# Four staging buffers for the memory keys and one junk tile of their own for the samples' scores

## Chip, cores and metric

The kernel runs on one core of a Trainium2 chip. The metric is the device time of one execution in microseconds (us). Three runs of the kernel before took 849.76, 850.98 and 851.43 us; their median, 850.98 us, is the time before.

## What is computed

One decoder layer for a prompt of 512 tokens and 8 samples of one token each, so 520 columns in all. Three sub-layers follow each other: a mixer (mLSTM and retention heads), a cross-attention of 4 heads into 256 memory tokens, and a SwiGLU feed-forward. The change touches the cross-attention. There, the prompt attends to keys and values that are made from `mem_prompt` in this kernel and are outputs too; each sample attends to its own cached keys and values, which come from memory.

```
def mem_kv(mem, g_mem, w_ck, w_cv):
    mn = rmsnorm(mem, g_mem)
    k = (mn @ w_ck).reshape(B, N_MEM, X_HEADS, X_HEAD_DIM)
    v = (mn @ w_cv).reshape(B, N_MEM, X_HEADS, X_HEAD_DIM)
    return k, v

def cross_attn(x, mk, mv, w_cq, w_co):
    q = (x @ w_cq).reshape(B, T, X_HEADS, X_HEAD_DIM)
    s = jnp.einsum('bthd,bmhd->bhtm', q, mk) * (X_HEAD_DIM ** -0.5)
    p = jax.nn.softmax(s, axis=-1)
    o = jnp.einsum('bhtm,bmhd->bthd', p, mv).reshape(B, T, D_MODEL)
    return o @ w_co
```

## The kernel before

Activations lie feature-major: 128 features on the partitions, 520 columns, 8 blocks of 128 features. Every float32 operand of a matmul is split into a rounded part (hi, by ScalarE) and the rest (lo, by VectorE), and each product is three matmuls (hi·hi, hi·lo, lo·hi). Weights come in 140 pieces of up to 512 KB through `wload`: SyncE loads `wraw` (3 buffers), ScalarE casts `whi` (2 buffers), VectorE subtracts `wlo` (2 buffers); for the pieces in `LO_ON_POOL` (52 to 55 and 60 to 71, the first half of the memory values' weights, the later queries' and those of the output projection) GpSimd does the subtraction instead.

The order of the instructions on each engine is not the order of the code: the program is built with a scheduler that simulates a timeline and fixes one order per engine beforehand. On the chip each engine then runs its list in order and waits on semaphores. So a change of buffers, which changes who must wait for whom, also changes the orders.

The cross-attention in the order of the code:

- `queries(h)` makes two blocks of queries (`pcq`, `qf`), and `ask(h)` turns the samples' queries into `Mq`.
- `mem_keys(cb)`, eight times: 24 matmuls into PSUM (`pmk`, one of the two buffers of the pool `acc`), VectorE scales them into the staging tile `kf` (L887), `split` makes KT hi on ScalarE and KT lo on VectorE, and GpSimd issues the DMA that writes `kf` out as the output of the memory keys (L889).
- `mem_values(c)`, twice: 48 matmuls of 512 columns into `pmv` (pool `acc` too).
- `samples()`, a coroutine beside all this: for every cached tile (`kv`, 512 KB, 3 buffers, loaded by SyncE) a unit `keys` or `values`. A unit has two matmuls that spread a query or a weight row over the partitions (`pq` or `pw`, one of four PSUM buffers of the tag `msc`, which `pxs`, `ppT`, `pxo`, `pst` and `ptq` share in turn), and four VectorE instructions (L953 or L967, each followed by the read of its accumulator) that multiply tile and row and keep only the sum; the product itself goes to a junk tile `jk` that nobody reads. There are 32 units, 16 of keys and 16 of values. After four keys of a head, `exps` transposes the scores (`pst`, L975), makes the softmax and, in `samples`, the rows `Mp` (L194) that the values of that head need. After four values, a split of `sv` writes the sample columns of `B` (hi on ScalarE, lo on VectorE, L191).
- `heads()` does the prompt's attention (`pxs`, `ppT`, `pT`, `pxo`), and the passes of the output projection (`pwc`, L222) add into `X` (L1128, the last pass L295). The first pass needs the rows of heads 0 and 1 in `B`, the second those of head 2, the third those of head 3, each with the samples' columns.

The staging tile and the junk tiles share one tag in the pool `cp`, whose tiles have two buffers unless told otherwise: `kf` in `mem_keys`, `jk` (`sjk`) in `keys` and `jk` (`svj`) in `values` take turns in two buffers.

```
kf = cp.tile([P, NM], F32, tag="kf", name="kf")          # mem_keys
jk = cp.tile([P, XD], F32, tag="kf", name="sjk")         # keys
jk = cp.tile([P, NM], F32, tag="kf", name="svj")         # values
```

Of the kernel before, what the change touches and what calls it, by code (L numbers as in the profile page):

```python
# [10 lines left out]
F32 = mybir.dt.float32  # L11
# [12 lines left out]
P = 128  # L24
# [8 lines left out]
NM = 256  # L33
XD = 256
# [106 lines left out]
def decoder_step(ctx: ExitStack, tc: tile.TileContext, i: dict, o: list):  # L141
# [20 lines left out]
    def ps2(name):  # L162
        return acc.tile([P, 2, 512], F32, tag="acc", name=name)

    def ps1(name):
        return psums[-1].tile([P, 512], F32, tag="msc", name=name)
# [17 lines left out]
    def selb(b):  # L184
        return sel[:, 4 * P + b * P : 4 * P + (b + 1) * P]


    def split(hi, lo, src, scale=None):

        if scale is None:  # L190
            return act.copy(hi, src), dve.tensor_tensor(lo, src, hi.bitcast(F32), ALU.subtract)  # L191
        else:
            act.activation(hi, src, AF.Copy, scale=scale)
            dve.scalar_tensor_tensor(lo, src, scale, hi.bitcast(F32), ALU.mult, ALU.subtract)  # L194
# [18 lines left out]
    def mm3(out, wh, wl, xh, xl, first, last):  # L213
        pe.matmul(out, wh, xh, start=first, stop=False)
        pe.matmul(out, wh, xl, start=False, stop=False)
        pe.matmul(out, wl, xh, start=False, stop=last)
# [15 lines left out]
    def step():  # L232

        for t in list(tasks):
            t[1] -= 1
            if t[1] <= 0:
                try:
                    t[1] = next(t[0]) or 2
                except StopIteration:
                    tasks.remove(t)  # L240
# [583 lines left out]
    cp = cx.enter_context(tc.tile_pool(name="cp", bufs=2))  # L824
# [53 lines left out]
    def mem_keys(cb):  # L878

        hi, lo = W.get()  # L880
        pk = ps2("pmk")[:, 0]
        for k in range(KB):
            mm3(pk[:, :NM], hi[:, k], lo[:, k], memh[:, k], meml[:, k], k == 0, k == KB - 1)
            if k in (2, 5):
                step()
        kf = cp.tile([P, NM], F32, tag="kf", name="kf")
        dve.tensor_tensor(kf, pk[:, :NM], rm_bc, ALU.mult)  # L887
        split(KT[:, 0, cb], KT[:, 1, cb], kf)
        pool.dma_start(mk_o[cb], kf)  # L889
        step()  # L890
# [41 lines left out]
    def cache_tile():  # L932

        while cached and len(loaded) < 3:
            src, h, b2 = cached.pop(0)
            t = cp.tile([P, 4, XD], F32, tag="kv", name="kv", bufs=3)
            sp.dma_start(t, src[h, b2])
            loaded.append(t)
        return loaded.pop(0)
# [3 lines left out]
    def keys(t, sc):  # L943

        kc = cache_tile()
        pq = ps1("pq")
        jk = cp.tile([P, XD], F32, tag="kf", name="sjk")
        for b1 in range(2):
            pe.matmul(pq[:, b1 * XD : (b1 + 1) * XD], selb(t * 2 + b1), Mq, start=True, stop=True)
        for b1 in range(2):  # L950
            b = t * 2 + b1
            for m in range(2):
                dve.tensor_tensor_reduce(  # L953
                    jk, kc[:, b1 * 2 + m], pq[:, b1 * XD : (b1 + 1) * XD], 1.0, 0.0, ALU.mult, ALU.add, sc[:, m, b : b + 1]
                )

    def values(t, sv):

        vc = cache_tile()
        pw = ps1("pw")  # L960
        jk = cp.tile([P, NM], F32, tag="kf", name="svj")
        for b1 in range(2):
            pe.matmul(pw[:, b1 * NM : (b1 + 1) * NM], selb(t * 2 + b1), Mp, start=True, stop=True)
        for b1 in range(2):
            b = t * 2 + b1
            for dd in range(2):
                dve.tensor_tensor_reduce(  # L967
                    jk, vc[:, b1 * 2 + dd], pw[:, b1 * NM : (b1 + 1) * NM], 1.0, 0.0, ALU.mult, ALU.add, sv[:, dd, b : b + 1]
                )
# [14 lines left out]
    def samples():  # L984
# [4 lines left out]
        for t in range(4):  # L989
            keys(t, sc)  # L990
            yield SAMPLES_REST[0]
# [3 lines left out]
        for h, units in enumerate(ORDER):  # L995
            split(Mp[0:8], Mp[32:40], e[0], scale=e[1])
            yield 1
            sc = cp.tile([P, 2, NS], F32, tag="ssc", name="ssc")
            sv = cp.tile([P, 2, NS], F32, tag="sv", name="sv")
            at = {"V": 0, "K": 0}  # L1000
            for z in units:
                while z == "K" and asked[0] <= h:
                    yield 1
                (values if z == "V" else keys)(at[z], sv if z == "V" else sc)
                at[z] += 1
                if z == "V" and at[z] == 4:
                    kb = 2 * h
                    split(B[:, 0, kb : kb + 2, T:], B[:, 1, kb : kb + 2, T:], sv)
                    done[0] = h
                yield SAMPLES_REST[h + 1]  # L1010
                if z == "K" and at[z] == 4:
                    scored[0] = h + 1
                    e = exps(sc)
                    if z == units[-1]:
                        yield 3
# [88 lines left out]
    for cb in range(KB):  # L1104
        mem_keys(cb)
# [289 lines left out]
```

## Time and profile before

| | us |
|---|---|
| median of three runs | 850.98 |
| the profiled execution | 851.71 |
| its span, first to last instruction | 849.9 |
| TensorE (PE) busy | 824.3, 97% of the span |
| VectorE (DVE) busy | 632.8, 74% |
| ScalarE (ACT) busy | 426.5, 50% |
| GpSimd (POOL) busy | 163.0, 19% |

The memory keys are made between 323 and 352 us, the memory values up to 385, the remaining queries up to 418, the output projection up to 481. The profile shows a TensorE clock of 1.00 of full speed in the stretches up to 464 us. A matmul's record is longer than its turn, since matmuls are pipelined: what a row costs is read from one start to the next. In the timelines a number in brackets is the idle time of the engine before a row and who ended it. Buffer numbers are left out of the names there, but the printed orders of the program have them, so that `pq_4851` in an order is one of the `pq` of the timeline.

### The profile page before, as it was taken

What the parts mean: (1) busy time and instruction counts of PE and PEld (TensorE: products, weight loads), DVE (VectorE), ACT (ScalarE), POOL (GpSimd) and SP (SyncE); (2) the same over time, 40 slices, a digit from 0 to 9 for tenths busy, and PEclk for the clock granted to TensorE, in tenths of its full rate; (3) what the DMA queues carried; (4) which work ended last, traced back from release to release, by engine and by line L of the source; (5) the groups of instructions that cost most, each with busy time, mean ns of one, the idle gap of its engine ahead of it and who ended that gap; (6) DMA issues with size and microseconds to landing.
All of it is one profiled execution on the core that took longest, in us unless ns stands there. A gap on an engine that the chain in (4) does not pass through costs nothing.

```text
span 849.9 us, 16985 instructions
## 1 busy us (share of the span) xinstructions
PE 824.3 (97%) x6643; PEld 807.6 (95%) x6643; DVE 632.8 (74%) x1393; ACT 426.5 (50%) x871; POOL 163.0 (19%) x282
## 2 busy tenths in 40 slices
PE   6999999999999999899999899999999999999995
PEld 4999999999999999789999899999999999999995
DVE  5999977667676778767888899999999997422234
ACT  6556886556545544356432555555454455332231
POOL 5122422222145301424322500000000000010010
PEclk9999999999999999999999999999999999999999
DMA  8344546444526347784755222333333333333212
GB/s 279 103 131 164 176 168 217 158 138 162 189 76 216 105 127 246 235 287 130 243 196 153 75 58 93 107 113 90 109 113 118 101 99 94 94 106 94 79 59 100
DMA packets 34088, 119.01 MB, mean 140 GB/s; under 512 B 4320, under 2 KB 6560, under 8 KB 32728
## 3 DMA queue, kind: packets, MB, share of 16 engines
q1 hardware_dynamic: 27216, 95.80, 35.9%
q0 software_dynamic: 5024, 20.79, 6.7%
q10 hardware_dynamic: 1768, 1.34, 0.5%
q8 instruction: 52, 0.85, 0.4%
q14 instruction: 28, 0.23, 0.1%
HBM read 108.77 MB, written 9.14 MB: 139 GB/s over the span
## 4 chain that ended last, share of the span: by engine, by line
PE 86%; DVE 6%; DMA 4%; POOL 1%; ACT 1%; issue 1%; SPq 0%; DVEq 0%; POOLq 0%; ACTq 0%
PE pfd L1277 13%; PE pfb L1236 6%; PE pfa L1236 6%; PE pcv L222 6%; PE pgt L222 5%; PE pcq L222 5%; PE pwo L222 5%; PE ppl L222 5%; PE pwc L222 4%; PE pfd L1236 3%; PE pfe L1236 3%; PE pfc L1236 3%; PE prp L222 3%; PE pfu L222 2%; PE pfg L222 2%; PE pfd L1317 1%
## 5 line engine op out<-in xcount | busy, mean ns | idle before, releaser
L207 ACT CAST whi<-wraw 128x1024 fp32r<-128x1024 f32 (+1 forms) x104 | 107.3, 1033 | 167.3 <-PE pfd L1277 58.1
L208 DVE TENSOR_TENSOR wlo<-wraw,whi 128x1024 fp32r<-128x1024 f32 (+1 forms) x88 | 112.6, 1281 | 71.5 <-ACT whi L207 69.5
L306 POOL TENSOR_TENSOR ssq<-ssq,sq 128x520 f32<-128x520 f32 x18 | 29.1, 1618 | 355.6 <-ACT sq L305 355.5
L191 ACT CAST qhi<-wsum 128x512 fp32r<-128x512 f32 x72 | 42.9, 620 | 41.4 <-DVE wsum L1183 26.6
L1277 PE MATMUL pfd<-TT,whi 128*128 128x260 f32 x392 | 62.8, 283 | 0.0
L1277 PEld LDWEIGHTS pfd<-TT,whi 128*128 128x128 f32 x392 | 53.7, 189 | 0.0
L1236 PE MATMUL pfa<-TT,qhi 128*128 128x260 f32 x288 | 53.1, 282 | 0.0
L1236 PE MATMUL pfb<-TT,qhi 128*128 128x260 f32 x288 | 52.8, 283 | 0.0
L208 POOL TENSOR_TENSOR wlo<-wraw,whi 128x1024 fp32r<-128x1024 f32 x16 | 38.4, 2399 | 60.3 <-ACT whi L207 55.2
L191 DVE TENSOR_TENSOR qlo<-wsum,qhi 128x512 fp32r<-128x512 f32 x72 | 48.9, 683 | 0.6 <-ACT qhi L191 0.6
L222 PE MATMUL pwc<-B,whi 128*128 128x260 f32 x256 | 43.8, 287 | 4.0 <-DVE X L295 3.0
L222 PE MATMUL pcv<-A,whi 128*128 128x260 f32 x256 | 44.3, 293 | 1.7 <-ACT whi L207 1.7
L1236 PEld LDWEIGHTS pfb<-TT,qhi 128*128 128x128 f32 x288 | 44.4, 189 | 0.2 <-issue 0.2
L1236 PEld LDWEIGHTS pfa<-TT,qhi 128*128 128x128 f32 x288 | 44.4, 189 | 0.0
L222 PE MATMUL prp<-A,whi 128*128 128x260 f32 x256 | 44.2, 291 | 0.0
L222 PE MATMUL ppl<-A,whi 128*128 128x260 f32 x256 | 42.9, 287 | 0.0
L222 PE MATMUL pgt<-A,whi 128*128 128x260 f32 x256 | 42.7, 289 | 0.0
L222 PE MATMUL pcq<-A,whi 128*128 128x260 f32 x256 | 42.0, 284 | 0.0
L222 PE MATMUL pwo<-B,whi 128*128 128x260 f32 x256 | 41.4, 283 | 0.0
L1236 PE MATMUL pfb<-TT,qlo 128*128 128x260 f32 x144 | 40.8, 283 | 0.0
L222 PEld LDWEIGHTS pwc<-B,whi 128*128 128x128 f32 x256 | 35.8, 189 | 5.1 <-DVE X L295 3.7
L1236 PE MATMUL pfa<-TT,qlo 128*128 128x260 f32 x144 | 40.5, 282 | 0.0
(431 smaller groups left out, 2556.6 us busy)
## 6 DMA issues: line engine op xcount, KB each, us to landing
wraw<-in_weights_dram SPq DMA_DIRECT2D x132, 512.0 KB, 3.8
kqb<-there POOLq DMA_DIRECT2D x8, 1024.0 KB, 5.2
kv<-in_cache_k_dram SPq DMA_DIRECT2D x16, 512.0 KB, 4.3
kv<-in_cache_v_dram SPq DMA_DIRECT2D x16, 512.0 KB, 4.4
wraw<-in_weights_dram SPq DMA_DIRECT2D x8, 384.0 KB, 3.1
X<-in_x_dram SPq DMA_DIRECT2D x2, 1040.0 KB, 5.9
Cs<-in_state_C_dram POOLq DMA_DIRECT2D x4, 512.0 KB, 4.3
out_dram<-Cs POOLq DMA_DIRECT2D x4, 512.0 KB, 3.0
```

The source lines that it names most:

```text
L191: return act.copy(hi, src), dve.tensor_tensor(lo, src, hi.bitcast(F32), ALU.subtract)
L207: act.copy(hi[:, :n], raw[:, :n])
L208: (pool if index in LO_ON_POOL else dve).tensor_tensor(lo[:, :n], raw[:, :n], hi[:, :n].bitcast(F32), ALU.subtract)
L222: pe.matmul(ps[:m, a, :H2], w[:, k, c0 : c0 + m], x[:, s, xk, a * H2 : (a + 1) * H2], start=first and w is hi and s == 0, stop=last and w ...
L306: (dve if ob == KB - 1 else pool).tensor_tensor(ssq, ssq, s, ALU.add)
L1236: pe.matmul(out, w[:, k * P : (k + 1) * P], x[:, k * H2 : (k + 1) * H2], start=k == 0 and w is wh and x is xh, stop=k == 3 and w is wl,)
L1277: pe.matmul(ps[:, a, :H2], w[:, k - k0], ff(s, k, slice(a * H2, (a + 1) * H2)), start=k == 0 and w is hi and s == 0, stop=k == FB - 1 and ...
L1317: pe.matmul(ps, w[:, k], ff(s, k0 + k, ts), start=k0 + k == 0 and w is hi and s == 0, stop=k0 + k == FB - 1 and w is lo,)
```

## The change

The staging tile `kf` gets four buffers. The junk tiles of both kinds get a tag of their own, `jk`, with one buffer.

```diff
-        kf = cp.tile([P, NM], F32, tag="kf", name="kf")
+        kf = cp.tile([P, NM], F32, tag="kf", name="kf", bufs=4)
...
-        jk = cp.tile([P, XD], F32, tag="kf", name="sjk")
+        jk = cp.tile([P, XD], F32, tag="jk", name="sjk", bufs=1)
...
-        jk = cp.tile([P, NM], F32, tag="kf", name="svj")
+        jk = cp.tile([P, NM], F32, tag="jk", name="svj", bufs=1)
```

No instruction is added or taken away; the orders of all engines change between the third memory key and the end of the output projection. Three places follow. The names: `kf`, `sjk`, `svj`, `KT` as above, `snb`, `spp` and `Mp` belong to the samples' softmax, and what stands in brackets is what the instruction waits for (DMASW: a DMA issued by GpSimd, DMAHW: one issued by SyncE or ScalarE, DVE: VectorE itself).

First place: VectorE at the fifth and sixth memory key, before.

```order
L967 ISA svj_4592,sv_4588<-kv_4407,pw_4591 128x256 [waits DMAHW3_49,DMASW2_49,PE_49]
L967 ISA sv_4588 128x1
L887 TENSOR_TENSOR kf_4605<-pmk_4566,rm_bc_3547 128x256 [waits DMASW3_49]
L208 TENSOR_TENSOR wlo_4659<-wraw_4656,whi_4658 128x1024 [waits DMAHW1_49,Activation_49]
...
L887 TENSOR_TENSOR kf_4641<-pmk_4616,rm_bc_3547 128x256 [waits DMASW4_49]
L953 ISA sjk_4649,ssc_4587<-kv_4464,pq_4648 128x256 [waits DMAHW6_49,DVE_49,PE_49]
```

The same engine with the change, from the seventh key's staging to the first scores behind the eighth:

```order
L887 TENSOR_TENSOR kf_4687<-pmk_4662,rm_bc_3547 128x256 [waits DMASW2_49,PE_49]
L191 TENSOR_TENSOR KT_3545<-kf_4687,KT_3545 128x256 [waits Activation_49]
L967 ISA svj_4592,sv_4588<-kv_4407,pw_4591 128x256 [waits DMAHW3_49,PE_49]
...
L887 TENSOR_TENSOR kf_4733<-pmk_4698,rm_bc_3547 128x256 [waits DMASW3_49,PE_49]
L967 ISA svj_4592,sv_4588<-kv_4407,pw_4591 128x256 [waits DVE_49]
L967 ISA sv_4588 128x1
L967 ISA svj_4592,sv_4588<-kv_4407,pw_4591 128x256 [waits DVE_49]
L967 ISA sv_4588 128x1
L191 TENSOR_TENSOR KT_3545<-kf_4733,KT_3545 128x256 [waits Activation_49]
L953 ISA sjk_4649,ssc_4587<-kv_4464,pq_4648 128x256 [waits DMAHW6_49,DVE_49]
```

A `kf` now waits for the DMA of the fourth one before it, and no score waits for such a DMA. The unit `svj_4592`, which stood between the fourth and the sixth `kf`, stands around the eighth, and the unit `sjk_4649` behind the last KT.

Second place: VectorE at the first values of head 2, before.

```order
L967 ISA svj_5639,sv_5606<-kv_5470,pw_5638 128x256 [waits DMAHW0_49,PE_49]
L967 ISA sv_5606 128x1
L967 ISA svj_5610,sv_5606<-kv_5448,pw_5609 128x256 [waits DVE_49]
L967 ISA sv_5606 128x1
L967 ISA svj_5639,sv_5606<-kv_5470,pw_5638 128x256 [waits DVE_49]
L967 ISA sv_5606 128x1
```

With the change:

```order
L967 ISA svj_5610,sv_5606<-kv_5448,pw_5609 128x256 [waits DVE_49]
L967 ISA sv_5606 128x1
L967 ISA svj_5639,sv_5606<-kv_5470,pw_5638 128x256 [waits DMAHW0_49,DVE_49,PE_49]
L967 ISA sv_5606 128x1
L967 ISA svj_5639,sv_5606<-kv_5470,pw_5638 128x256 [waits DVE_49]
L967 ISA sv_5606 128x1
```

Two units took turns before, so that a score's wait was for a product two scores back; now they stand one behind the other, and every score waits for the one just before it, that of the next unit too.

Third place: TensorE at the last softmax of the samples (`pst_5816`), before.

```order
L222 MATMUL pwc_5890<-B_81,wlo_5762 128x260
L975 MATMUL pst_5816<-cst_85,ssc_5605 8x128
L222 MATMUL pwc_5890<-B_81,wlo_5762 128x260
L222 MATMUL pwc_5890<-B_81,whi_5761 128x260 x3
L975 MATMUL pst_5816<-cst_85,ssc_5605 8x128
L963 MATMUL pw_5827<-Mp_4069,sel_86 128x256 x2
L222 MATMUL pwc_5890<-B_81,whi_5761 128x260
```

With the change:

```order
L222 MATMUL pwc_5947<-B_81,wlo_5762 128x260 x2
L222 MATMUL pwc_5997<-B_81,whi_5886 128x260
L975 MATMUL pst_5816<-cst_85,ssc_5605 8x128 x2
L963 MATMUL pw_5827<-Mp_4069,sel_86 128x256 x2
L963 MATMUL pw_5850<-Mp_4069,sel_86 128x256 x2
L222 MATMUL pwc_6011<-B_81,whi_5886 128x260
L214 MATMUL pxo_5860<-pT_5788,Vm_3546 128x512
```

The second `pst` stood behind 159 matmuls of the output projection; it stands behind 193 now, when the whole first pass (`pwc_5947` is its last block) is issued.

## Rows read from the trace of the kernel before

**Rows 1.** Stretches: busy us of PE, PEld, DVE, ACT, POOL; clock, DMA share, GB/s.

```profile
323.00:352.00 29.00, 26.64 (x214) 25.57 (x213) 23.69 (x59) 12.22 (x20) 5.89 (x8) 1.00 0.77 244
418.00:445.00 27.00, 27.00 (x219) 26.27 (x218) 22.66 (x78) 12.03 (x27) 8.58 (x4) 1.00 0.62 200
```

**Rows 2.** Waits of PE in the whole span: us in total, times, longest.

```profile
PE pwc L222 <- DVE X L295: 3.0, 2, 2.7
PE pmk L214 <- DVE kf L887: 1.6, 2, 1.5
PE pwc L222 <- DVE X L1128: 0.9, 2, 0.7
PE pq L949 <- DVE ssc L953: 0.7, 1, 0.7
```

**Rows 3.** Timeline of PE at the last memory keys: start, us, instruction.

```profile
342.25 0.40 PE L949 MATMUL pq<-Mq,sel 128*128 128x256 f32 x2
342.81 0.39 PE L214 MATMUL pmk<-B,whi 128*128 128x256 f32 x1 [0.16 <-DVE kf L887]
...
345.78 0.40 PE L963 MATMUL pw<-Mp,sel 128*128 128x256 f32 x2
347.65 0.36 PE L214 MATMUL pmk<-B,whi 128*128 128x256 f32 x1 [1.47 <-DVE kf L887]
...
350.48 0.28 PE L216 MATMUL pmk<-B,wlo 128*128 128x256 f32 x1
351.45 0.51 PE L949 MATMUL pq<-Mq,sel 128*128 128x256 f32 x2 [0.70 <-DVE ssc L953]
352.07 0.47 PE L214 MATMUL pmv<-whi,B 128*128 128x512 f32 x1
```

**Rows 4.** Chain that ended last, one piece: start, us, what (matmuls of `pwc`).

```profile
461.03 8.91 PE pwc L222 x72
```

**Rows 5.** Timeline of DVE at the last memory keys.

```profile
347.08 0.42 DVE L887 TENSOR_TENSOR kf<-pmk,rm_bc 128x256 f32<-128x256 f32 x1 [1.72 <-DMA out_dram<-kf]
347.42 0.41 DVE L953 CUSTOM_DVE_ANT_0 sjk<-kv,pq 128x256 f32<-128x256 f32 x1
...
347.87 0.42 DVE L953 CUSTOM_DVE_ANT_0 sjk<-kv,pq 128x256 f32<-128x256 f32 x1
...
348.68 2.38 DVE L191 TENSOR_TENSOR KT<-kf,KT 128x256 fp32r<-128x256 f32 x1
```

**Rows 6.** Timeline of POOL in the same stretch.

```profile
347.80 0.54 POOL L889 DMA_DIRECT2D out_dram<-kf  x1 [4.21 <-DVE kf L887]
348.35 2.42 POOL L208 TENSOR_TENSOR wlo<-wraw,whi 128x1024 fp32r<-128x1024 f32 x1
```

**Rows 7.** Timeline of DVE where two units of values take turns.

```profile
430.69 0.42 DVE L967 CUSTOM_DVE_ANT_0 svj<-kv,pw 128x256 f32<-128x256 f32 x1
...
431.03 0.42 DVE L967 CUSTOM_DVE_ANT_0 svj<-kv,pw 128x256 f32<-128x256 f32 x1
```

**Rows 8.** Timeline of PE: first `pw` of head 2, second `pst` of the last softmax, second pass.

```profile
428.23 0.40 PE L963 MATMUL pw<-Mp,sel 128*128 128x256 f32 x2
...
444.14 0.27 PE L975 MATMUL pst<-cst,ssc 128*8 128x128 f32 x1
...
452.90 0.35 PE L222 MATMUL pwc<-B,whi 128*128 128x260 f32 x1
```

**Rows 9.** Timeline of DVE: last key score to the splits of the outputs.

```profile
441.62 0.42 DVE L953 CUSTOM_DVE_ANT_0 sjk<-kv,pq 128x256 f32<-128x256 f32 x1
...
450.55 0.69 DVE L1128 TENSOR_TENSOR X<-X,pwc 128x520 f32<-128x520 f32 x1
451.16 0.41 DVE L967 CUSTOM_DVE_ANT_0 svj<-kv,pw 128x256 f32<-128x256 f32 x1
...
452.11 0.70 DVE L191 TENSOR_TENSOR B<-sv,B 128x16 fp32r<-128x16 f32 x1
...
463.38 0.17 DVE L191 TENSOR_TENSOR B<-sv,B 128x16 fp32r<-128x16 f32 x1
```

## Prediction

> **What bounds the kernel now.** Read the stretches first [rows 1]: from 418 to 445 us TensorE (PE) is busy all the time, and VectorE (DVE) over eight tenths of it. At the memory keys, 323 to 352 us, PE has free time, 2.4 us of 29. So the chip follows PE's list, and a DVE instruction counts only where PE has to wait for it. The list of PE's waits says where that is [rows 2]: on the staging `kf` 1.6 us, on a sample's score 0.7 us, both at the memory keys, and then on the additions into `X`, 0.9 and 3.0 us, in the output projection.
>
> The timeline of PE at the keys gives the sizes [rows 3]. A matmul's turn is 0.124 us, 72 of them in 8.91 us [rows 4]. From 342.25 to 342.81 two matmuls need 0.25 of 0.56 us; from 345.78 to 347.65 two need 0.25 of 1.87; from 350.48 to 351.45 one needs 0.12 of 0.97; from there to 352.07 two need 0.25 of 0.62. PE loses 0.3 + 1.6 + 0.85 + 0.4 = 3.2 us (rounded). The cause is in DVE's timeline [rows 5]: `kf` stood 1.72 us for a DMA that writes out an earlier `kf`, since two buffers serve `kf` and the junk of the scores. The scores queued behind it ended late, and with them the PSUM buffer that PE's next `pq` takes over.
>
> There is a second chain, that of the samples: scores, softmax, `Mp`, values, split. It meets PE again at the second pass of the output projection. The lo split of head 2's outputs runs from 452.11 to 452.81 us [rows 9], and the next matmul of that pass starts at 452.90 [rows 8]. So in this trace PE is not early there: what it gains before 452 us is worth something only if the samples come earlier too.
>
> **The change, part by part.**
>
> *Four staging buffers.* Each `kf` now waits for the DMA issued four keys before; a key takes PE 24 x 0.124 = 3.0 us, so that DMA is some 12 us old, where one of a single key before came 1.72 us too late [rows 5]. The waits on DMAs go, at the scores too. Upper bound of the gain: the 3.2 us above. Lower bound: nothing, if another wait takes the place at once.
>
> *What is late next.* In the new order the unit `sjk_4649` stands behind the last KT split, and PE takes its PSUM buffer for `pq_4851` after 12 matmuls of the memory values. I follow both with the rows' durations. Without stalls the eighth key ends near 347.7 us, and PE stands at `pq_4851` near 351.2. On DVE the last `kf` follows PE's end, two scores and the KT split follow it, and then four scores at 0.46 us each: the last is done near 351.9. PE waits about 0.7 us, so 2.5 of the 3.2 us are left. Bounds: no wait, and the case of the second rival.
>
> *One junk buffer.* A score that follows another unit's score starts 0.34 us after it (430.69 to 431.03 [rows 7]); one that waits for the write just before it starts 0.46 us after (347.87 less 347.42 is 0.45 [rows 5]). So such a wait costs 0.12 us of DVE. In the order before 27 of the 128 scores follow a score that wrote the same buffer; with the change it is 66, since two units no longer take turns. That is 39 x 0.12 = 4.7 us more on DVE, 19 of the 39 (2.3 us) behind the first values of head 2. What covers them is the free time of DVE, 4.3 us from 418 to 445 [rows 1]; where a score is on the chain of the samples there is no cover. The Trainium skill, in "VectorE: DVE Perf Modes", section "The DRAIN you can't avoid", says that a semaphore between chained VectorE operations costs nothing extra, as the pipe is emptied anyway. The rows here disagree, with 0.34 against 0.45 us. By that page the sum below would be 0.5 us less.
>
> *The order of PE.* The scheduler now puts the samples' work later between PE's matmuls: `pst_5816` stands behind 193 matmuls `pwc`, not 159. PE works through its list, so these 34 x 0.124 = 4.2 us stand before the last softmax, whether its scores are ready or not. Less the 2.5 us gained, the second `pst` comes at 444.14 + 4.2 - 2.5 = 445.8 us [rows 8]. Are the scores of the keys ready then? The first `pw` of head 2 has 17 matmuls more in front, so it comes at 428.23 + 2.1 - 2.5 = 427.8; from there to the last key score DVE took 13.4 us (441.62 less 428.23 [rows 8, 9]), and now 10 waits of 0.12 and one more addition into `X`, 0.6 us (451.16 less 450.55 [rows 9]): 15.2 us, so 443.0. They are ready; PE's list decides.
>
> *From `pst` to the split of head 2's outputs.* Before it took 452.81 - 444.14 = 8.7 us. One addition into `X` and a split of `pT`, 0.6 us each, now stand ahead of it or hide in PE's time: -1.2. Four more waits: +0.5. The split itself, 16 columns wide, took 0.70 us, and the one of the next head 0.17 [rows 9]: -0.5. That gives 7.5 us: the split ends at 453.3, 0.5 us later than before.
>
> *The end.* Behind it, the second pass is the same on PE. The 0.9 us that PE waited there for additions into `X` [rows 2] may go, as PE then comes later than DVE; on the other side, the split of the last head's outputs is put behind the last addition of the pass, so PE waits for an addition and a small split, 0.8 us, less four matmuls that it can do first: +0.4. The third pass and all behind it keep their order, so I take no change there, the waits of 3.0 us [rows 2] included.
>
> Sum: -3.2 + 0.7 (kept at the keys) + 4.2 (order of PE) - 1.2 + 0.5 - 0.5 (shorter chain) - 0.9 + 0.4 = 0.0 us. The whole is a large gain that is handed back. The profiled execution, 851.71 us with a span of 849.9, is 0.7 us above the median of the runs; against the median the forecast is 851.0 us.
>
> **The rivals.**
>
> *The gain stays (faster).* The 4.2 us of PE's order cost nothing if PE really is that much earlier, that is if the samples' chain behind `pst` gets shorter by more than I take: the softmax's steps on ScalarE and DVE find both engines free, and DVE is not held by GpSimd. For it speaks that at the keys the change takes away just the wait that the rows show, and that DVE has free time. Against it: the lo split and PE's next matmul meet at 452.8 us already. The time if 2.7 of the 3.2 us are kept: 848.3 us. It decides if the split of head 2 ends before 451 us.
>
> *The last KT split is held by GpSimd (slower).* At 348.68 this split took 2.38 us; the one of GpSimd's `wlo`, 2.42 us long, had begun at 348.35 [rows 5, 6]. With the change the last KT split stands behind two scores: it is ready about 0.7 us after the end of `kf`. GpSimd issues the DMA of that `kf` (it began 0.3 us after the end of `kf`, and took 0.54 us) and then begins the next `wlo`, about 0.85 us after the end [rows 5, 6]. If GpSimd is first, the KT split and the four scores behind it are late by 2.38 - 0.42 = 2.0 us (0.42 is `kf` itself [rows 5], as wide as the split), and the split before it can lose as much to the `wlo` before. PE then waits at `pq_4851` not 0.7 but 2.7 to 3.5 us; nothing of the gain at the keys is left, and the 4.2 us of PE's order stand unpaid. The sum is then +2.0 to +2.8; I take +2.4: 853.4 us. It decides from the point where PE's gain at the first memory values is under 0.8 us. The margin is 0.15 us, so this is no unlikely case. The Trainium skill, in "SBUF — State Buffer", section "Who interferes with whom", says that a VectorE instruction with two SBUF inputs and a GpSimd instruction that reads SBUF take one shared port by turns and that the one that begins first holds it to its end; the rows agree, the split ended at 351.06, just behind the `wlo` at 350.77.
>
> *The change does nothing.* The waits on the DMAs are gone from the order, so this one is small; its time is the one of before, and it counts to the forecast's side.
>
> **How the numbers follow.** About 0.2% of the time, 1.7 us, is what a measurement of this kernel can tell from no change. The forecast, within 1.7 us of 850.98, has 0.45 with the third rival; the slower rival 0.32; the faster one 0.23. The likeliest gives 851.0 us; its own range, with PE's wait at `pq_4851` between 0 and 2 us and the 0.9 us kept or not, is 849.5 to 852.7. The range for 8 in 10 reaches into both rivals: 849.0 leaves the core of the faster one out, 853.7 takes most of the slower one in.
>
> **What would show it.** Right would be: no PE wait on `kf`; the memory values begin near 348 us and not at 352; a wait of PE on a score at the first chunk of the memory values; the pair of `pst` of the last softmax near 446 us, with a gap of PE behind it, and a split of head 2's outputs that ends near 453 us; from the third pass on the same distances as before. Wrong: the split at 450 us or earlier (the first rival), a KT split of over 2 us behind the last `kf` and a PE wait of 3 us there (the second), or PE waits on `kf` as before (the third).

## The result and the profile after

The change is slower: 862.66 us (858.13 to 868.18, five runs) against 851.15 for the kernel before on the same chip, ratio 1.0129, 95% interval 1.0099 to 1.0158. The forecast was 851.0, its range ended at 853.7.

The profiled execution took 861.76 us, 10.05 more than that of before. TensorE (PE) begins the memory keys 1.6 us later, at 324.69 and not 323.08; ahead of that its order is the same in both, and over all profiled runs below this start lies anywhere between 320.9 and 326.7 us, so I don't put it down to the change. From there to the first matmul of the feed-forward part (`pfg`, at 480.99 before, 491.40 after) it is 157.9 us before and 166.7 after: **8.8 us are lost in this stretch**. Behind it the two are equal within 0.4 us. I use this stretch for the experiments too, since it leaves out what varies ahead of it.

The waits of PE in it, after the change (in total, times, longest; before: the four of [rows 2] and no others of 0.2 us or more; in the whole span of the kernel before there are longer ones that [rows 2] doesn't show, the longest 6.6 us on `A`, ahead of the keys):

```profile
PE pq L949 <- DVE ssc L953: 5.7, 1, 5.7
PE pw L963 <- DVE Mp L194: 2.1, 1, 2.1
PE pwc L222 <- DVE X L295: 2.0, 1, 2.0
PE pwc L222 <- DVE B L191: 1.6, 1, 1.6
PE pwc L222 <- DVE X L1128: 0.7, 1, 0.7
PE pxo L214 <- DVE pT L191: 0.2, 1, 0.2
```

The waits on `kf` are gone, as the change promises. But the one on a sample's score went from 0.7 to 5.7 us, and there are new ones on `Mp` and on a split into `B`. The sums are 6.2 us before and 12.3 after, 6.1 more. The rest is in the clock, as PE's timeline at the long wait shows:

```profile
352.03 0.39 PE L215 MATMUL pmv<-wlo,B 128*128 128x512 f32 x1
352.25 0.39 PE L216 MATMUL pmv<-whi,B 128*128 128x512 f32 x1
...
352.72 0.40 PE L963 MATMUL pw<-Mp,sel 128*128 128x256 f32 x2
358.85 0.80 PE L949 MATMUL pq<-Mq,sel 128*128 128x256 f32 x2 [5.73 <-DVE ssc L953]
...
359.87 0.63 PE L216 MATMUL pmv<-whi,B 128*128 128x512 f32 x1
360.30 0.63 PE L214 MATMUL pmv<-whi,B 128*128 128x512 f32 x1
...
363.71 0.41 PE L216 MATMUL pmv<-whi,B 128*128 128x512 f32 x1
```

Before the wait one `pmv` follows another after 0.22 us, behind it after 0.43, up to 363.71. The stretches of PE give the granted clock (busy us of PE, PEld, DVE, ACT, POOL; clock, DMA share, GB/s):

```profile
323.00:352.00 29.00, 29.00 (x234) 28.40 (x233) 25.04 (x62) 13.63 (x22) 6.90 (x10) 1.00 0.77 250
352.00:359.00 7.00, 1.27 (x7) 0.90 (x5) 6.86 (x12) 1.05 (x1) 4.75 (x3) 0.85 0.43 133
359.00:362.00 3.00, 3.00 (x8) 2.42 (x9) 2.70 (x13) 0.00 (x0) 0.00 (x0) 0.50 0.75 216
```

At the keys PE is now busy all of the 29 us (26.64 before [rows 1]). Then it stands, and from the wait's end to 363.71 it works at 0.50, the lower of its two levels, 1.2 GHz: half of 4.86 us is 2.4 us lost. 6.1 + 2.4 = 8.5 of the 8.8 us. The clock is at 0.50 at the end of the stretch too, for 1.4 us after the change and 0.5 before, which is some 0.4 us more.

Why the score came so late stands in DVE's timeline:

```profile
347.17 2.92 DVE L191 TENSOR_TENSOR KT<-kf,KT 128x256 fp32r<-128x256 f32 x1 [0.62 <-ACT KT L191]
...
350.81 0.42 DVE L887 TENSOR_TENSOR kf<-pmk,rm_bc 128x256 f32<-128x256 f32 x1
...
351.95 5.12 DVE L191 TENSOR_TENSOR KT<-kf,KT 128x256 fp32r<-128x256 f32 x1
356.99 0.41 DVE L953 CUSTOM_DVE_ANT_0 sjk<-kv,pq 128x256 f32<-128x256 f32 x1
...
358.37 0.42 DVE L953 CUSTOM_DVE_ANT_0 sjk<-kv,pq 128x256 f32<-128x256 f32 x1
```

and in that of GpSimd (POOL):

```profile
347.41 2.39 POOL L208 TENSOR_TENSOR wlo<-wraw,whi 128x1024 fp32r<-128x1024 f32 x1
351.53 0.56 POOL L889 DMA_DIRECT2D out_dram<-kf  x1 [1.73 <-DVE kf L887]
352.12 4.66 POOL L208 TENSOR_TENSOR wlo<-wraw,whi 128x1024 fp32r<-128x1024 f32 x2
```

The last split of `KT`, 0.42 us by itself, took 5.12: it ended at 357.07, just behind the second of two low halves (352.12 + 4.66 = 356.78; a low half is here GpSimd's subtraction that makes the `wlo` of one weight piece). Four scores follow it, and PE waits for the last of them. The split before it was held in the same way (2.92 us, to 350.09; the low half to 349.80). At the end of the stretch it happens to a split 16 columns wide, where PE's 1.6 us on `B` are:

```profile
475.25 2.32 DVE L191 TENSOR_TENSOR B<-sv,B 128x16 fp32r<-128x16 f32 x1 [0.29 <-ACT B L191]
```

```profile
475.19 2.35 POOL L208 TENSOR_TENSOR wlo<-wraw,whi 128x1024 fp32r<-128x1024 f32 x1 [3.32 <-ACT whi L207]
```

The same split without a low half beside it took 0.17 us [rows 9].

What exposes a split is its second tile in SBUF; one whose source lies in PSUM is not held. Two splits of `pT` (128x512, from `ppT` in PSUM) ran one behind the other in the change while a low half began, and took 0.68 us each, 1.28 together, as they do alone:

```profile
430.47 1.28 DVE L191 TENSOR_TENSOR pT<-ppT,pT 128x512 fp32r<-128x512 f32 x2
```

```profile
431.06 2.41 POOL L208 TENSOR_TENSOR wlo<-wraw,whi 128x1024 fp32r<-128x1024 f32 x1 [3.42 <-ACT whi L207]
```

In the thirteen traces (both kernels and the runs below), from 320 to 495 us, 87 splits (L191) with both inputs in SBUF overlap a low half in time. 85 of them took longer than alone; the other two met only its last 0.2 us. None of the 195 that met no low half did. Of the splits from PSUM 24 began while a low half ran, and none took longer.

### The profile page after: what moved, and what is told of

It reads as the page before. It is cut to its first block, busy times and chain, and to the rows that moved or that the text cites. A ratio compares the mean times of both kernels' runs of the same rounds, so it can differ in the third digit from the quotient of the medians.

```text
span 860.0 us, 16988 instructions
## 1 busy us (share of the span) xinstructions
PE 827.4 (96%) x6643; PEld 810.7 (94%) x6643; DVE 643.5 (75%) x1393; ACT 425.4 (49%) x871; POOL 162.0 (19%) x282
## 5 line engine op out<-in xcount | busy, mean ns | idle before, releaser
L191 ACT CAST qhi<-wsum 128x512 fp32r<-128x512 f32 x72 | 43.0, 621 | 41.0 <-DVE wsum L1183 26.6
L191 DVE TENSOR_TENSOR qlo<-wsum,qhi 128x512 fp32r<-128x512 f32 x72 | 48.8, 682 | 0.6 <-ACT qhi L191 0.6
```

## The experiments

**Theory:** the change is slower because the new order lets DVE's splits, which read two tiles in SBUF, meet GpSimd's low halves, and they are held until those end. **Rivals:** the order of PE and the one junk buffer make the scores late, whoever makes the low halves; or the four staging buffers matter by themselves. "Stretch" is the time from the first matmul of the keys to the first `pfg`, in the profiled execution. It is one execution of each kernel, before included; the ratios come from all executions. In runs 2 and 8 the stretch is 8.4 and 6.1 us longer than before's, and the ratios are worth 4.6 and 3.0 us. So the stretch tells where time goes, and the ratio how much.

**1. Two staging buffers again.** `name="kf", bufs=4` back to `bufs=2`, the junk buffer kept.

> The change with the memory keys' staging tile at two buffers again, the one junk buffer kept. The order of the instructions on all five engines is the same as with four buffers, row by row. Theory (the order that goes with the junk buffer of its own puts the last two splits of the memory keys beside GpSimd's low halves, and the splits are held until those end): same time as the change, 860 to 864 us; two splits of KT of 2.9 and 5.1 us, a wait of TensorE at the queries' matmul of 5 to 6 us, half the clock behind it. Rival (the four buffers themselves matter): with two, a staging tile is given back too late, TensorE waits 1 to 3 us more on the memory keys (862 to 866), or, if the four buffers cost something, the time falls back towards 851.

Ratio to before 1.0099 (1.0068 to 1.0130), stretch 166.5 us, splits of 2.92 and 5.12 us, the same list of waits. The number of staging buffers, four or two, does nothing that can be measured once the junk has its own tile; the loss, and the gain at the keys (24.5 us from the first to the last `pmk`, as in the change), come from taking the junk out of the shared tile.

**2. Two junk buffers.** `name="sjk", bufs=1` and `name="svj", bufs=1` to `bufs=2`.

> The change with two junk buffers of their own. Theory (it is the single junk buffer, by the order it leads to, that costs; the four staging buffers are good for the 3 us that TensorE lost at the memory keys): no split held by two of GpSimd's low halves, the wait at the queries' matmul under 2 us, no fall of the clock behind it, 848 to 853 us. Rival (any junk buffer apart from the staging tiles' lets DVE run the splits late, or four staging buffers harm): a split of KT over 4 us again, 858 to 863.

A miss: ratio 1.0054 (1.0026 to 1.0081), stretch 166.3 us. The long wait is gone, and others stand in its place (the largest five of PE):

```profile
PE pwc L222 <- DVE X L295: 3.0, 2, 2.7
PE pxs L214 <- DVE sv L967: 2.3, 1, 2.3
PE pw L963 <- DVE Mp L194: 2.0, 1, 2.0
PE pwc L222 <- DVE X L1128: 1.8, 1, 1.8
PE pmv L215 <- POOL wlo L208: 1.6, 1, 1.6
```

In this order too two splits of `KT` are held, 2.61 and 2.51 us, each by one low half; PE takes over another PSUM buffer behind them. The clock is at 0.50 twice for 3.4 us, behind the waits on `X`. So the loss doesn't need the single junk buffer. That the held splits make it here too is what run 10 tests.

**3. One low half of the pair to DVE.** `LO_ON_POOL` without 53.

> The change with one of GpSimd's low halves (weight 53, the first of the pair that ran back to back beside the last split of KT) moved to DVE. Theory: the last split of KT takes 0.4 us (at most 2.4, if another low half meets it), the 5.7 us wait goes to under 1.5, the clock behind it stays at 1.00; 5.7 - 1 + 2.4 regained less 1.2 us on DVE that stands before the scores: 853 to 857 us. Rival (TensorE waits because one junk buffer and the order put the scores late, whoever makes the low half): the wait stays at 4 us or more, 859 to 863.

Ratio 1.0014 (0.9984 to 1.0045), stretch 161.1 us: no difference from before is left that can be measured. DVE:

```profile
352.82 0.42 DVE L191 TENSOR_TENSOR KT<-kf,KT 128x256 fp32r<-128x256 f32 x1
```

GpSimd's next low half now begins at 353.60, and PE's `pq` has no wait (355.83, with 12 more matmuls of the values ahead of it):

```profile
355.83 0.40 PE L949 MATMUL pq<-Mq,sel 128*128 128x256 f32 x2
```

The clock stays at 1.00 here. It fell elsewhere in this run, behind the 2.1 us on `Mp`, for 3.4 us (1.7 us lost), where the same wait in the change was not followed by a fall.

**4. The last low half to DVE.** `LO_ON_POOL` without 71; PE's and ACT's orders are unchanged.

> The change with GpSimd's last low half (weight 71, beside the last split of the samples' values) moved to DVE; TensorE's and ACT's orders are the same row by row, on DVE one row is added just before that split. Theory: the split of 128x16 takes 0.17 us in place of 2.32, behind a low half of 1.2 us, so TensorE's third pass starts about 1 us sooner: 860.5 to 862.5 us. Rival (the third pass waits on something else): the wait of 1.6 us stays or grows by up to 1.2, 862 to 864.

Ratio 1.0062 (1.0031 to 1.0094), stretch 165.0 us, the wait on `B` from 1.6 to 0.5:

```profile
PE pwc L222 <- DVE B L191: 0.5, 1, 0.5
```

The 1.1 us of the wait are what the theory forecast. The median is 2.3 us below that of run 1, which has the change's order and ran on the same chip in the same set; the intervals are too wide to tell 2.3 from 1.1.

**5. Both.** `LO_ON_POOL` without 53 and 71.

> The change with both of GpSimd's low halves (weights 53 and 71) moved to DVE: the edits of the two runs before added up. Theory (held splits are what makes the change slower): from the first matmul of the memory keys to the first of the feed-forward part the change took 166.7 us, the one edit 161.1, the other 165.0; added 159.4, and 157.7 where the clock does not fall behind TensorE's wait on Mp; before it was 157.9. Time 0 to 2 us above before's in the same call. Rival (the loss moves to another place): the stretch stays at 161 or more, 3 us or more above before.

Stretch 159.8 us, with 1.7 us of half clock behind the wait on `Mp`; ratio 1.0011 (0.9986 to 1.0037). The two add up as expected.

**6. And the last head's values one yield later.** `yield 1` behind the split into `Mp` becomes `yield 2 if h == 3 else 1`.

> As the run with both low halves on DVE, and the last head's values yield once more after their Mp, so that TensorE's list has the six matmuls of the second pxo ahead of the pw that waits for Mp. Theory (TensorE's list puts pw too early: it waits 2.1 us with 1.4 us of ready work behind it): the wait on Mp goes to about 0.7 us, no fall of the clock behind it, 1.4 us less than the run with both low halves, 156.3 to 158 us for the stretch, at or up to 1.5 us below before. Rival (the last head's values then come later, and the third pass waits for their split): the wait moves there, the same time.

Half a hit: the wait on `Mp` went to 0.7 us and the clock stayed up, but 0.9 us now go to a split into `B`. Stretch 158.6 us, ratio 0.9995 (0.9973 to 1.0018).

**7. Four shared buffers.** Before, with `bufs=4` for `kf`, `sjk` and `svj` under the one tag.

> Before with four buffers for the shared tag: staging tiles and junk take turns among four, none has a buffer of its own. Theory (the gain at the memory keys, some 3 us, can be had with any number of buffers above two, but the order follows from the number and decides where splits meet GpSimd's low halves): no wait of TensorE on staging, the stretch from memory keys to feed-forward 155 to 160 us if at most one split on the path is held, above 163 if two are. Rival (more buffers are better as such): 154 to 156, 2 to 4 us faster than before.

The longest stretch of all: 170.4 us, ratio 1.0125 (1.0088 to 1.0161). Two splits of `KT` (2.79 and 2.85 us) and two of `sv` (2.30 and 1.96 us) are held, and PE waits where they end; the wait on `kf`, which the theory expected gone, is still there, with 1.2 us. That more buffers are better as such is out.

**8. The low half ahead of the pair to DVE.** `LO_ON_POOL` without 52. PE's order is that of the change row by row, so this tells the theory from the rival best.

> The change with the low half before the pair (weight 52) moved to DVE. TensorE's order is that of the change row by row. Theory (the wait of 5.7 us is the last KT split held to the end of two low halves): the pair on GpSimd then starts about 350.5 us after its own timing of the change, one low half sooner or not at all beside that split; held by one, the split takes 2.4 us, and the wait goes to about 2 us; held by none it goes to under 1; stretch 160 to 164 us. Rival (TensorE's order and the one junk buffer make the wait): same order, so the wait stays at 5 to 6 us and the stretch at 166 to 167.

DVE, and then GpSimd:

```profile
351.26 2.70 DVE L191 TENSOR_TENSOR KT<-kf,KT 128x256 fp32r<-128x256 f32 x1
```

```profile
351.27 2.40 POOL L208 TENSOR_TENSOR wlo<-wraw,whi 128x1024 fp32r<-128x1024 f32 x1
354.09 2.36 POOL L208 TENSOR_TENSOR wlo<-wraw,whi 128x1024 fp32r<-128x1024 f32 x1 [0.43 <-ACT whi L207]
```

```profile
355.74 0.51 PE L949 MATMUL pq<-Mq,sel 128*128 128x256 f32 x2 [2.38 <-DVE ssc L953]
```

Now 0.43 us lie between the two low halves, and the split gets through: it is held by one, and the wait is 2.4 us instead of 5.7. Stretch 164.0 us, ratio 1.0035 (1.0013 to 1.0057). The order of PE alone does not make the 5.7 us. The clock was at 0.50 behind this wait, behind that on `Mp` and at the end, 3.4 us each.

**9. No low half on GpSimd at the keys and values.** `LO_ON_POOL = set(range(60, 71))`, with the yield of run 6.

> The change with all four low halves of the keys and values stage (weights 52 to 55) and the last one (71) on DVE, and the last head's values one yield later. Theory: no split of KT takes more than 0.5 us, TensorE has no wait over 1 us but the 2.0 on X at the end, 155.5 to 158 us from memory keys to feed-forward, 0 to 2.5 us faster than before. Rival (DVE, with 4 x 1.23 us more, becomes late itself): waits of TensorE on DVE of 2 us and more at the memory values, 159 to 163.

**Faster than both kernels:** 850.48 us, ratio 0.9957 (0.9938 to 0.9976), stretch 157.0 us. All eight splits of `KT` take 0.42 us, and the waits of PE are

```profile
PE pwc L222 <- DVE X L295: 2.0, 1, 2.0
PE pwc L222 <- ACT B L191: 0.9, 1, 0.9
PE pw L963 <- DVE Mp L194: 0.5, 1, 0.5
```

and four more of 0.4 us or less. The ratio is worth 3.7 us (2.0 to 5.3), more than the expected 2.5 at most; the stretch is only 0.9 us shorter than that of before, so these two traces don't show where the rest comes from.

**10. The same edits on run 2.**

> The run with two junk buffers, with weights 52 to 55 and 71 on DVE and the last head's values one yield later. Theory (what that run lost, 166.3 us for the stretch, it lost to held splits, 2.3 at the first scores of a head, 1.6 at the memory values, 1.8 on X and the clock behind that): those waits go, 156 to 159.5 us, at before's time or up to 2 us below. Rival (two junk buffers spread the scores badly by themselves): 162 or more.

Ratio 0.9974 (0.9946 to 1.0002), stretch 156.4 us, the shortest of all: run 2's 166.3 us less 9.9. Its waits at `pxs` (2.3) and at `pmv` (1.6) are gone.

**11. Before, without those four low halves on GpSimd.**

> Before with the four low halves of the keys and values stage (weights 52 to 55) on DVE. Theory: the split of KT of 2.38 us goes to 0.4, TensorE's 0.7 us behind a score goes, its 1.6 us on staging stay, stretch 156.5 to 158, no difference that can be measured. Rival (DVE, with 4 x 1.23 us more, becomes late): 159 to 162.

Ratio 1.0019 (0.9996 to 1.0042), stretch 160.8 us: longer, though no split of `KT` is held any more. But the reason is not the rival's. DVE again stands for a DMA of the shared tile, and PE behind it, with half the clock for 3.4 us:

```profile
352.41 0.42 DVE L887 TENSOR_TENSOR kf<-pmk,rm_bc 128x256 f32<-128x256 f32 x1 [2.06 <-DMA out_dram<-kf]
```

So moving these low halves alone brings nothing, and the junk's own buffer alone costs 1.0% (run 1); the two together, with the later yield and weight 71 as in run 9, gain. Before with these last two edits as well was not run, so how much of run 9's gain is theirs is not shown.

## Why the prediction was wrong

*Four staging buffers (-3.2 us).* The mechanism was right, the size a little low. From the first `pmk` to the first `pmv` (352.07 before [rows 3], 349.30 after) PE took 28.99 us before for 212 matmuls and 24.61 after for 206:

```profile
349.30 0.40 PE L214 MATMUL pmv<-whi,B 128*128 128x512 f32 x1
```

Six matmuls are 0.7 us, so some 3.6 us are gained. And the four buffers had no part in it (run 1).

*What is late next (a wait of 0.7 us at `pq_4851`).* **This is the step that failed.** It measured 5.7 us, and 2.4 of half clock behind it, for which no case had a price. The timing I worked out was good: I had the last split of `KT` ready 0.7 us after the end of `kf` and GpSimd's low half 0.85 us after it; the rows say 0.72 (351.95 less 351.23) and 0.89 (352.12). From that 0.15 us of margin I let the split go first. It did begin first, by 0.17 us, and was held all the same. The slower rival described what happened, and its price was for one low half, 2.0 us; two stood in GpSimd's queue, and as ScalarE's cast for the second had ended (353.77) before the first was done (354.49), nothing came between them. Its sum, with the wait of 2.7 us +2.0, becomes +5.0 with the wait of 5.7 and +7.4 with the clock; the larger gain at the keys makes it +7.0 or so, of 8.8 measured. The rest lies behind the keys (below) and in the clock at the end.

*One junk buffer (66 scores that wait for the write just before).* Right: 66 scores of the change stand 0.44 us or more behind a score directly ahead of them, and none under 0.4; before there were 36 under 0.4. What they cost in time was not measured by itself; with two junk buffers (run 10) 45 are under 0.4 again, and the stretch is only 0.6 us shorter than with one (run 9).

*The order of PE and the samples' chain (+4.2, then -1.2 + 0.5 - 0.5).* Right. The last softmax's transposes come at

```profile
455.01 0.38 PE L975 MATMUL pst<-cst,ssc 128*8 128x128 f32 x2
...
460.40 0.48 PE L963 MATMUL pw<-Mp,sel 128*128 128x256 f32 x2 [2.15 <-DVE Mp L194]
```

and head 2's split ends at 462.29:

```profile
462.12 0.17 DVE L191 TENSOR_TENSOR B<-sv,B 128x16 fp32r<-128x16 f32 x1
```

That is 7.17 us from the second `pst` (455.12), where I had 7.5. Less the 1.6 us of the later start and 7.4 of the long wait and its clock (5.7 - 0.7 + 2.4), the split ends at 453.3 us of the time before, as the prediction said.

*The end (-0.9 + 0.4, the third pass unchanged).* Near in the sum, wrong in the parts. All I forecast behind the keys adds to +2.5 us; the waits of PE there went from 3.9 us (0.9 + 3.0) to 6.6 (2.1 + 2.0 + 1.6 + 0.7 + 0.2), +2.7, and read from one start to the next, where a wait costs a little more than its idle time, PE lost some 3.7 us more than before. That the sum came near is luck: the additions into `X` kept 0.7 of their 0.9 us, and the third pass, where I took no change, lost 1.6 to a held split and got 1.0 back at its end. From start to start the whole is -3.6 at the keys, +5.9 for the long wait, +2.4 and +0.4 for the clock and +3.7 behind: the 8.8 us.

*The range.* 849.5 to 852.7 doesn't come out of the terms named for it: a wait of 0 to 2 us in place of 0.7, and 0.9 us kept or not, give 850.3 to 853.2. The clock behind a wait stood in no term.

*The rivals.* The first fell with the wait; the third was out, as the waits on the DMAs are gone. The second had 0.32 and the right place. Its chance rested on a margin of which the trace of before could not say how much is enough; I should have given it more than half, and priced it by everything GpSimd had ready.

## What to carry to other kernels

Where an edit moves a DVE instruction that reads two SBUF tiles next to GpSimd instructions that read SBUF too, its price is the end of the last of those that follow each other without a gap, not of one, and a lead in the timeline, up to 0.24 us here, doesn't save it. An edit of buffer counts in a program whose order is made by a scheduler is an edit of the order: look at what now stands beside what, before counting the waits that the buffers remove. Here the junk's own buffer took DVE off the DMA, and the low halves had to leave GpSimd where the splits then fell before anything was gained.

## What the runs showed that I had not expected

- *The first to begin is not the one that goes through.* The Trainium skill, in "SBUF — State Buffer", section "Who interferes with whom", says that whoever issues first gets the shared ports for the whole instruction. By the recorded starts the trace doesn't agree: DVE's split began 0.24 us (347.17 and 347.41) and 0.17 us (351.95 and 352.12) ahead of GpSimd's low half and was held to its end both times, as in run 7 with leads of 0.14 and 0.16 and in run 8 with 0.01. What the recorded start holds besides the instruction's reads these runs don't show.
- *Two of GpSimd's instructions back to back hold it through both*, 5.12 us; with 0.43 us between them it gets through after the first, 2.70 us (run 8).
- *The size hardly matters to the one held:* 16 columns took 2.32 us in place of 0.17. A held split ended 0.03 us (16 columns), 0.3 us (256) or 0.55 us (512) behind the low half, in all 85 cases.
- *The clock:* behind PE's 5.7 us of standing still it was at 0.50 for 4.9 us in the change, and it was 0.50 behind that wait in runs 1 and 4 too, and in run 8 for 3.4 us behind the wait of 2.4 us at the same place. Behind the 2.1 us on `Mp` it fell in runs 3, 5 and 8 and did not in the change and in runs 1, 2 and 4. So a wait of 2 us costs 2 us in one run and nearly 4 in another.
